# A hybrid decoder block in f32: a new order for the opening, for the weights at two stage borders, and for the gates

## The chip, the cores and the metric

The kernel runs on one core of one Trainium2 chip. The metric is the time of one execution on the device in microseconds (us), lower is better. Its engines are named as in the profile: PE (TensorE, with PEld for its weight loads), DVE (VectorE), ACT (ScalarE), POOL (GpSimd) and SP (SyncE, which here only issues loads and stores).

## The reference

One layer on 512 tokens of width 1024, all in f32: a gated feed-forward block (inner width 2816), a mixer, and a second feed-forward block, each with a norm ahead of it and behind it.

```python
f = swiglu(rmsnorm(x, ffn1_pre_g[l]), ffn1_w_gate[l], ffn1_w_up[l], ffn1_w_down[l])
x = x + 0.5 * rmsnorm(f, ffn1_post_g[l])
y = hybrid_mixer(rmsnorm(x, mix_pre_g[l]), positions, w_in[l], conv_w[l], conv_b[l], ...)
x = x + rmsnorm(y, mix_post_g[l])
f = swiglu(rmsnorm(x, ffn2_pre_g[l]), ffn2_w_gate[l], ffn2_w_up[l], ffn2_w_down[l])
x = x + 0.5 * rmsnorm(f, ffn2_post_g[l])
```

Here `rmsnorm(x, g) = x * rsqrt(mean(x*x) + 1e-6) * g` along the width, and `swiglu` is `(silu(h @ w_gate) * (h @ w_up)) @ w_down`. The mixer projects `h` once and feeds two branches: windowed attention with 3 groups of 4 heads (window and dilation 128/1, 512/4, 2048/16; q and k partly rotated), and a matrix memory (mLSTM) with 4 heads, whose input and forget gates are 8 more columns of the projection. Both are gated, added and projected by `w_out`.

## The kernel before

Tokens stand in 4 tiles `x0` to `x3` of 128 tokens. A normed tile `h` is transposed on PE and kept as features by tokens, split in two f32r parts: `hTh`, a rounded copy made by ACT, and `hTl`, the rest, made by DVE (`turn_norm`). Weights are split alike (`load_w`): SP loads a tile `wf` of 128x1024 (512 KB), ACT casts it to `wh`, DVE makes `wl = wf - wh`. A product in full precision is three: `wh` with `hTh`, `wh` with `hTl`, `wl` with `hTh`. `wf` has 3 buffers, `wh` and `wl` 5 each, so a load waits until DVE has made the `wl` of three tiles earlier, and a cast until PE has used the `wh` of five tiles earlier.

*Opening.* `x0`, the gain `f1pre` (spread over 128 partitions by its load), `x1`, the first block's gate and up weights (`agu00`, `agu01`), `x2`, `x3` and the next weights are loaded in this order by SP. `prenorm_first` squares and sums a tile on ACT, POOL takes the power -0.5, DVE scales by it and the gain. 28 products on zeros (`warm`) run on PE ahead. Then tiles 0 and 1 are transposed and split; the products of the first two of 22 inner blocks run over half the tokens at a time (`by_halves`): block 0 on tiles 0 and 1, then, at the places in `FLUSH`, the transposes of tile 2 and, within block 1, those of tile 3; then both blocks on tiles 2 and 3. Blocks 0 to 3 are plain products; the rest use a scheme with seven products for eight (`seven`), which needs sums of quarters of `h` (`token_parts`).

*Stage borders.* In `down`, the last products of a feed-forward block (and of `w_out`) are finished token tile by token tile: `PostNorm.bank` squares each half of a tile out of PSUM on ACT, and `prenorm` makes the next stage's `h`. The transposes of tiles 0 and 1 for the next stage are taken from `todo` between the products of the last two tiles. The next stage starts `by_halves` in the same way, with its first weights from `load_w`; all but the first are held by `tc.issue_after` until the transposes' copies are done.

*Gates.* The 8 gate columns come with group 0's values (`gts`). `gates()` transposes them on PE, then works on 4 rows of 512: two activations, an exponential and a logarithm on ACT (with a table load between them, and one back), and nine steps on DVE, two of them scans. It stands ahead of the loop over heads 1 to 3; in this loop each head projects q and k for its three groups (`qk_proj`, with the rotation in `qk_evac` on DVE), while the head before is finished (`exchange`, `turn`, `values`), and then computes its scores (`scores`). `gates_turn()`, eight narrow transposes, stands in head 1. `hg` and `selr` are two small tiles loaded by POOL that share buffers with the gates' temporaries.

The order on each engine is fixed when the program is built: a scheduler places the instructions by its own estimates, under the data's dependences and the `issue_after` pins; each engine then works strictly through its list.

Of the kernel before, what the change touches and what calls it, by code (L numbers as in the profile page):

```python
# [10 lines left out]
F32 = mybir.dt.float32  # L11
# [5 lines left out]
P = 128  # L17
# [17 lines left out]
WARM = 28  # L35
# [4 lines left out]
def tile_hybrid_block(ctx: ExitStack, tc: tile.TileContext, a: dict):  # L40
# [30 lines left out]
    for i in range(WARM):  # L71
        nc.tensor.matmul(wbank[:, 0:256], lhsT=warm[:, 0:P], rhs=warm, start=True, stop=True)
# [4 lines left out]
    nc.vector.memset(nhalf, -0.5)  # L77

    def load_w(src, name, n=1024, after=()):
        wf = act.tile([P, WMAX], F32, tag="wf", bufs=3, name=f"wf_{name}")[:, :n]  # L80
        nc.sync.dma_start(wf, src)
        with ExitStack() as st:
# [3 lines left out]
            nc.scalar.copy(wh, wf)  # L86
# [17 lines left out]

    def square(src, ss, b, name, half=False):
        junk = act.tile([P, 512], BF16, tag="junk", bufs=1, name=f"jk_{name}{b}")
        nc.scalar.activation(junk, src, AF.Square, scale=(2 if half else 1) * D ** -0.5, accum_out=ss[:, b:b + 1])
# [12 lines left out]
    def prenorm(t, g, where, name):  # L120
# [9 lines left out]
        return h  # L130

    def prenorm_first(t, g, where, after=None):
        h = scratch(f"h_f1{t}", *where)
        ss = small.tile([P, 2], F32, tag="ss", name=f"s1_{t}")[:, 0:1]
        with tc.issue_after(after) if after else nullcontext():
            nc.scalar.activation(h, xs[t], AF.Square, scale=D ** -0.5, accum_out=ss)
        nc.vector.tensor_scalar(ss, ss, EPS, None, op0=ALU.add)
        r = rsqrt(ss, 1, f"f1{t}")
        for c in BANKS:
            nc.vector.scalar_tensor_tensor(h[:, c], xs[t][:, c], r, g[:, c], op0=ALU.mult, op1=ALU.mult)  # L140
        return h
# [55 lines left out]
    def down(n, chunk_src, get_x, post, finish, todo, name, accs=None, first=0, late=lambda: None):  # L197
# [14 lines left out]
        for t in range(NT):  # L212
            pn = post(t)
            for b in range(2):
# [33 lines left out]

    def token_parts(low, tmp, hTh, hTl, name):
# [4 lines left out]
        for j in (1, 0):  # L254
            for i in (1, 0):
                nc.vector.tensor_tensor(quad(hf, i, j), quad(hTh, i, j).bitcast(F32), quad(hTl, i, j).bitcast(F32),
                                        op=ADD)
# [320 lines left out]
    def ffn(pool, todo, first_w, hT, wgu, wdq, wd, post, finish, name, begin=None, pins=()):  # L578
# [23 lines left out]
        for f in range(EARLY, PLAIN):  # L602
            w = load_plain(f)
# [668 lines left out]
```

## Time and profile before

| | |
|---|---|
| median of 3 runs | 1360.0 us (1359.94 to 1360.92) |
| the profiled execution | 1361.59 us, its span 1359.8 us |
| TensorE's granted clock, mean | 0.996 |
| ACT, POOL busy | 44%, 2% of the span |
| DMA | 145.91 MB, mean 107 GB/s |

Times in the profile count from the span's first instruction. A row of the timeline gives start, duration, engine, source line, operation and operands; a number in brackets is the time that the engine sat idle before it, and what ended it. Rows of PE's products overlap a little with their successors, since products are pipelined. In the list of waits, a row names the waiting engine and line, what was waited for, the sum, the number of times and the longest. A line of the stretches gives the stretch, the busy time of PE, PEld, DVE, ACT and POOL with counts of instructions, and then PE's clock, the share of busy DMA engines and GB/s.

### The profile page before, as it was taken

What the parts mean: (1) busy time and instruction counts of PE and PEld (TensorE: products, weight loads), DVE (VectorE), ACT (ScalarE), POOL (GpSimd) and SP (SyncE); (2) the same over time, 40 slices, a digit from 0 to 9 for tenths busy, and PEclk for the clock granted to TensorE, in tenths of its full rate; (3) what the DMA queues carried; (4) which work ended last, traced back from release to release, by engine and by line L of the source; (5) the groups of instructions that cost most, each with busy time, mean ns of one, the idle gap of its engine ahead of it and who ended that gap; (6) DMA issues with size and microseconds to landing.
All of it is one profiled execution on the core that took longest, in us unless ns stands there. A gap on an engine that the chain in (4) does not pass through costs nothing.

```text
span 1359.8 us, 19896 instructions
## 1 busy us (share of the span) xinstructions
PE 1344.6 (99%) x7976; PEld 1202.8 (88%) x7976; DVE 968.4 (71%) x1482; ACT 601.7 (44%) x969; POOL 30.1 (2%) x52
## 2 busy tenths in 40 slices
PE   8999999999999999999999999999999999999998
PEld 7899999878899889888888888888889999998786
DVE  7789898896772885675756754333378798997983
ACT  5444444555633532435545443222264444444552
POOL 1000000000200000000000000000010000000000
PEclk8999999999999999999999999999999999999999
DMA  5333333654233222222222232233213233335541
GB/s 201 94 109 95 109 109 109 232 171 150 69 93 123 78 78 91 81 78 78 78 78 78 78 108 79 95 107 100 95 47 116 94 94 108 109 104 194 174 150 62
DMA packets 40829, 145.91 MB, mean 107 GB/s; under 512 B 4652, under 2 KB 4652, under 8 KB 40736
## 3 DMA queue, kind: packets, MB, share of 16 engines
q1 hardware_dynamic: 39600, 141.08, 31.7%
q0 software_dynamic: 1136, 3.56, 0.8%
q8 instruction: 62, 1.02, 0.3%
q14 instruction: 31, 0.25, 0.1%
HBM read 142.53 MB, written 2.10 MB: 106 GB/s over the span
## 4 chain that ended last, share of the span: by engine, by line
PE 89%; DVE 6%; ACT 2%; issue 2%; DMA 1%; SPq 0%; DVEq 0%; POOLq 0%; ACTq 0%
PE p L176 11%; PE qb_b L319 9%; PE qb_a L319 9%; PE pq L176 8%; PE pm L176 6%; PE qa_b L319 4%; PE qa_a L319 4%; PE acc_o L227 3%; PE pvo L991 2%; PE pvo L993 2%; PE pvo L992 2%; PE pg_a L186 2%; PE pq L186 2%; PE pg_b L186 2%; PE pg_a L176 2%; PE pg_b L176 2%
## 5 line engine op out<-in xcount | busy, mean ns | idle before, releaser
L176 PE MATMUL pq<-hTh_mx,wh_qk 128*128 128x512 f32 x160 | 63.2, 395 | 0.0
L176 PE MATMUL pq<-hTl_mx,wh_qk 128*128 128x512 f32 x160 | 62.4, 390 | 0.0
L88 DVE TENSOR_TENSOR wl_qk<-wf_qk,wh_qk 128x1024 fp32r<-128x1024 f32 x24 | 29.3, 1221 | 41.6 <-ACT wh_qk L86 31.3
L176 PE MATMUL pm<-hTh_mx,wh_mqk 128*128 128x512 f32 x128 | 50.3, 393 | 0.0
L991 PE MATMUL pvo<-wh_vo,hTh_mx 128*128 128x512 f32 x128 | 50.2, 392 | 0.0
L176 PE MATMUL pm<-hTl_mx,wh_mqk 128*128 128x512 f32 x128 | 49.9, 390 | 0.0
L176 PE MATMUL p<-hTh_mx,wh_gm 128*128 128x512 f32 x128 | 49.9, 390 | 0.0
L993 PE MATMUL pvo<-wl_vo,hTh_mx 128*128 128x512 f32 x128 | 49.8, 389 | 0.0
L176 PE MATMUL p<-hTl_mx,wh_gm 128*128 128x512 f32 x128 | 49.8, 389 | 0.0
L992 PE MATMUL pvo<-wh_vo,hTl_mx 128*128 128x512 f32 x128 | 49.8, 389 | 0.0
L86 ACT CAST wh_qk<-wf_qk 128x1024 fp32r<-128x1024 f32 x24 | 25.0, 1045 | 56.1 <-PE pw L739 28.8
L1144 DVE SCALAR_TENSOR_TENSOR t<-t,p 128x512 f32<-128x512 f32 x16 | 11.0, 688 | 42.7 <-PE p L176 42.7
L88 DVE TENSOR_TENSOR wl_mqk<-wf_mqk,wh_mqk 128x1024 fp32r<-128x1024 f32 x16 | 19.6, 1223 | 29.7 <-ACT wh_mqk L86 25.3
L176 PE MATMUL pq<-hTh_mx,wl_qk 128*128 128x512 f32 x160 | 39.6, 389 | 0.0
L882 DVE SCALAR_TENSOR_TENSOR z<-pm,cw,z 128x511 f32<-128x511 f32 (+2 forms) x48 | 35.3, 743 | 1.4 <-ACT z L880 0.9
L319 PE MATMUL qa_a<-hTl_f,wh_a 128*128 128x256 f32 x144 | 36.1, 283 | 0.0
L319 PE MATMUL qa_b<-hTl_f,wh_b 128*128 128x256 f32 x144 | 36.1, 283 | 0.0
L319 PE MATMUL qa_a<-hTh_f,wh_a 128*128 128x256 f32 x144 | 36.1, 283 | 0.0
L319 PE MATMUL qa_b<-hTh_f,wh_b 128*128 128x256 f32 x144 | 36.1, 283 | 0.0
L247 ACT CAST wh_a<-cd_a 128x1024 fp32r<-128x1024 f32 x18 | 18.9, 1050 | 38.9 <-DVE cd_a L247 38.9
L247 ACT CAST wh_b<-cd_b 128x1024 fp32r<-128x1024 f32 x18 | 18.9, 1050 | 37.8 <-DVE cd_b L247 37.8
L176 PEld LDWEIGHTS pq<-hTh_mx,wl_qk 128*128 128x128 f32 x160 | 30.0, 188 | 6.2
(677 smaller groups left out, 4421.1 us busy)
## 6 DMA issues: line engine op xcount, KB each, us to landing
wf_qk<-in_wqk SPq DMA_DIRECT2D x24, 512.0 KB, 3.7
B_a<-in_wdq SPq DMA_DIRECT2D x21, 512.0 KB, 4.1
B_b<-in_wdq SPq DMA_DIRECT2D x21, 512.0 KB, 3.9
g_a<-in_wgu SPq DMA_DIRECT2D x18, 512.0 KB, 3.8
u_a<-in_wgu SPq DMA_DIRECT2D x18, 512.0 KB, 3.8
g_b<-in_wgu SPq DMA_DIRECT2D x18, 512.0 KB, 3.8
u_b<-in_wgu SPq DMA_DIRECT2D x18, 512.0 KB, 3.7
wf_mqk<-in_wmqk SPq DMA_DIRECT2D x16, 512.0 KB, 3.3
```

Of the source, the lines that this page charges most:

```text
L86: nc.scalar.copy(wh, wf)
L88: nc.vector.tensor_tensor(wl, wf, wh.bitcast(F32), op=ALU.subtract)
L176: nc.tensor.matmul(out, lhsT=wt[:, k * P:(k + 1) * P], rhs=x[:, k, tok], start=n == 0, stop=n == len(terms) - 1)
L186: nc.tensor.matmul(outs[b][:, tok], lhsT=ws_[b][w][:, k * P:(k + 1) * P], rhs=x[:, k, tok], start=i + k + hf == 0, stop=hf == 1 and i == 2 ...
L227: nc.tensor.matmul(out, lhsT=x[:, tk], rhs=w[:, cs], start=first and n == 0, stop=last and n == 2, skip_group_check=True)
L247: self.last[eng] = getattr(getattr(nc, eng), fn)(*args, **kw).ins
L319: nc.tensor.matmul(out, lhsT=wt[:, i * P:(i + 1) * P], rhs=y[:, i, :], start=first and n == 0, stop=last and n == len(terms) - 1, skip_gro ...
L882: nc.vector.scalar_tensor_tensor(z[:, s:], src[:, :T - s], cw[:, ct, 3 - s:4 - s], z[:, s:], op0=ALU.mult, op1=ALU.add)
L991: nc.tensor.matmul(out, lhsT=hTh[:, k, tk], rhs=wh[:, cs], start=k == 0, stop=False)
L992: nc.tensor.matmul(out, lhsT=hTl[:, k, tk], rhs=wh[:, cs], start=False, stop=False)
L993: nc.tensor.matmul(out, lhsT=hTh[:, k, tk], rhs=wl[:, cs], start=False, stop=k == KD - 1)
L1144: nc.vector.scalar_tensor_tensor(t1[:, b, :], t1[:, b, :], 1.0, p2[b], op0=ALU.add, op1=ALU.mult)
```

## The change

There are three parts.

*Opening.* The gain is loaded as one row of 4 KB by ACT's queue, and PE spreads it: two f32 products of a column of ones with the row put it in PSUM on all partitions, from where DVE reads it for tiles 0 and 1; ACT copies it to SBUF for tiles 2 and 3. The order of ACT and DVE is written out with `Order`. The 28 products on zeros become 34: `WARM` asks for 12 ahead of the row's products, 6 behind them, 10 behind tile 0's transposes and 6 behind tile 1's; in the built program two of the second group stand with the first, 14 and 4.

```diff
-WARM = 28
+WARM = (12, 6, 10, 6)
...
-        load_x(0)
-        g_pre = gain(a["ffn1_pre_g"], "f1pre", eng=nc.sync)
-        load_x(1)
+        row = work.tile([1, D], F32, name="f1pre_row")
+        ones = work.tile([1, P], F32, name="ones_row")
+        nc.vector.memset(ones, 1.0)
+        nc.scalar.dma_start(row, a["ffn1_pre_g"].rearrange("(o d) -> o d", o=1))
...
+        fill(WARM[0])
+        gp = pair("g_f1pre")
+        for b, c in enumerate(BANKS):
+            nc.tensor.matmul(gp[b], lhsT=ones, rhs=row[:, c], start=True, stop=True)
+        fill(WARM[1])
...
+        ss = [opening_square(t) for t in range(2)]
+        opening_power(0, ss[0])
+        opening_scale(0, 0, gp[0])
+        opening_power(1, ss[1])
+        for t, b in ((0, 1), (1, 0), (1, 1)):
+            opening_scale(t, b, gp[b])
+        whs = [opening_cast(0)]
+        turned = opening_turn(0)
+        for x in turned:
+            opening_high(*x)
+        whs.append(opening_cast(1))
+        turned += opening_turn(1)
...
```

ACT's list from the first square on, before (`h_f10` and `h_f11` are tiles 0 and 1, `wh_agu00` and `wh_agu01` the first two weights, `pt_f10_0` a bank of transposes):

```order
L136 ACTIVATE h_f10_130,s1_0_131<-x0_114 128x1024
L136 ACTIVATE h_f11_152,s1_1_153<-x1_115 128x1024
L86 CAST wh_agu00_176<-wf_agu00_174 128x1024
L151 CAST hTh_f1_128<-pt_f10_0_138 128x4x128
L151 CAST hTh_f1_128<-pt_f10_1_139 128x4x128
L151 CAST hTh_f1_128<-pt_f11_0_160 128x4x128
L151 CAST hTh_f1_128<-pt_f11_1_161 128x4x128
L86 CAST wh_agu01_182<-wf_agu01_180 128x1024
L136 ACTIVATE h_f12_188,s1_2_189<-x2_116 128x1024
L136 ACTIVATE h_f13_196,s1_3_197<-x3_117 128x1024
```

The same place after the change:

```order
L248 ACTIVATE h_f10_132,s1_0_136<-x0_86 128x1024
L248 ACTIVATE h_f11_133,s1_1_138<-x1_87 128x1024
L248 CAST wh_agu00_150<-wf_agu00_102 128x1024
L248 CAST hTh_f1_130<-pt_f10_0_152 128x4x128
L248 CAST hTh_f1_130<-pt_f10_1_153 128x4x128
L248 CAST wh_agu01_174<-wf_agu01_103 128x1024
L248 CAST hTh_f1_130<-pt_f11_0_176 128x4x128
L248 CAST hTh_f1_130<-pt_f11_1_177 128x4x128
L248 ACTIVATE h_f12_134,s1_2_198<-x2_88 128x1024
L248 COPY g_f1pre_200<-g_f1pre_0_120 128x512
L248 COPY g_f1pre_200<-g_f1pre_1_121 128x512
L248 ACTIVATE h_f13_135,s1_3_203<-x3_89 128x1024
```

The cast of the second weight moved ahead of tile 1's copies, and the gain's two copies stand between the squares of tiles 2 and 3. On DVE, the first sum of `token_parts` (`aT_a` from `hTh` and `hTl`) now stands ahead of the first two `wl`, with tile 2's small addition; before, both stood behind them.

*Stage borders.* `down` takes a function `ahead`, which calls `load_w` for the next stage's first two weights; the norm's first half of the last token tile is then pinned behind the second weight's cast. The other early weights are pinned behind a square of the last tile as well.

```diff
-                pn.bank(accs[t], b)
+                if (t, b) == (3, 0) and ahead:
+                    with tc.issue_after(ahead(pins[2:])):
+                        pn.bank(accs[t], b)
+                else:
+                    pn.bank(accs[t], b)
             finish(t)
-        return pins[2:]
+        return pins[2:] + squares[-3:-2]
...
+        def ahead1(pins):
+            wq0.extend(load_w(a["wqk"][0, 0, b], f"qk00{b}", after=pins if b else ()) for b in range(2))
+            return last_cast[0]
```

ACT's list at the first border, before (`wh_qk001` is the mixer's second weight, `jk_pf130` and `jk_pf131` the squares of the last token tile's halves, `h_mx2` the scaling of tile 2):

```order
L151 CAST hTh_mx_3743<-pt_mx1_0_3825 128x4x128
L107 ACTIVATE jk_mx21_3801,ss_mx2_3798<-x2_116 128x512
L151 CAST hTh_mx_3743<-pt_mx1_1_3826 128x4x128
L107 ACTIVATE jk_pf130_3839,sp_f13_3812<-accb_a3_2865 128x512
L129 ACTIVATE h_mx2_3797<-h_mx2_3797,r_mx2_3805 128x512
L86 CAST wh_qk001_3920<-wf_qk001_3918 128x1024
L107 ACTIVATE jk_pf131_3854,sp_f13_3812<-accd_a3_2861 128x512
L86 CAST wh_qk010_3926<-wf_qk010_3924 128x1024
L86 CAST wh_qk011_3932<-wf_qk011_3930 128x1024
```

The same place after the change:

```order
L148 CAST hTh_mx_3758<-pt_mx1_0_3840 128x4x128
L114 ACTIVATE jk_mx21_3816,ss_mx2_3813<-x2_88 128x512
L148 CAST hTh_mx_3758<-pt_mx1_1_3841 128x4x128
L91 CAST wh_qk001_3862<-wf_qk001_3860 128x1024
L137 ACTIVATE h_mx2_3812<-h_mx2_3812,r_mx2_3820 128x512
L114 ACTIVATE jk_pf130_3866,sp_f13_3827<-accb_a3_2880 128x512
L114 ACTIVATE jk_pf131_3881,sp_f13_3827<-accd_a3_2876 128x512
L91 CAST wh_qk010_3941<-wf_qk010_3939 128x1024
L91 CAST wh_qk011_3947<-wf_qk011_3945 128x1024
```

The cast changed places with the first square. At the second border (`ahead2`) the list changes in the same way, with `wh_bgu01` and `jk_pmx30`. SP's list of loads is the same as before but for the gain.

*Gates.* `gates()` and the load of `hg` move into head 1, behind its `turn`, and `gates_turn()` into head 2.

```diff
-    gates()
...
         pT = turn(h - 1, sm)
         if h == 1:
+            gates()
+            hg = work.tile([P, 1, D], F32, tag="gain", bufs=2, name="hg")
+            nc.gpsimd.dma_start(hg[:, 0, :], a["mlstm_head_g"].partition_broadcast(P))
+        elif h == 2:
             gates_turn()
```

DVE's list in head 1, before, around the rotation of its group 2 (`qk_12`; `sw_120` and `sw_121` are the swapped parts for q and k; `ga`, `gb4`, `gc4`, `selr` and `Gl` are the gates' rows):

```order
L724 TENSOR_TENSOR sw_111_4886<-sw_111_4886,ropeS_3897 32x512
L88 TENSOR_TENSOR wl_qk210_5167<-wf_qk210_5163,wh_qk210_5165 128x1024
L725 TENSOR_TENSOR qk_11_4879<-qk_11_4879,sw_111_4886 32x512
L88 TENSOR_TENSOR wl_qk211_5173<-wf_qk211_5169,wh_qk211_5171 128x1024
L722 STREAM_SHUFFLE sw_120_4989<-qk_12_4988 32x512
L723 TENSOR_TENSOR qk_12_4988<-qk_12_4988,ropeC_3896 32x512
L724 TENSOR_TENSOR sw_120_4989<-sw_120_4989,ropeS_3897 32x512
L725 TENSOR_TENSOR qk_12_4988<-qk_12_4988,sw_120_4989 32x512
L88 TENSOR_TENSOR wl_qk220_5266<-wf_qk220_5262,wh_qk220_5264 128x1024
```

The same place after the change:

```order
L811 TENSOR_TENSOR qk_11_4868<-qk_11_4868,sw_111_4875 32x512
L1007 SCALAR_TENSOR_TENSOR ga_4690<-gc4_4692 4x512
L1010 SCALAR_TENSOR_TENSOR ga_4690<-gc4_4692,ga_4690 4x512
L1012 SCALAR_TENSOR_TENSOR gb4_4691<-gc4_4692,ga_4690 4x512
L1013 TENSOR_TENSOR gb4_4691<-ga_4690,gb4_4691 4x512
L1014 SCALAR_TENSOR_TENSOR gc4_4692<-gb4_4691 4x512
L93 TENSOR_TENSOR wl_qk211_5178<-wf_qk211_5174,wh_qk211_5176 128x1024
L1015 CAST selr_4693<-gc4_4692 4x512
L1017 TENSOR_TENSOR gb4_4691<-gb4_4691,gc4_4692 4x512
L1016 TENSOR_TENSOR Gl_4694<-gc4_4692,selr_4693 4x512
L808 STREAM_SHUFFLE sw_120_4994<-qk_12_4993 32x512
L809 TENSOR_TENSOR qk_12_4993<-qk_12_4993,ropeC_3923 32x512
```

The gates' steps now stand between the rotations of groups 1 and 2 of head 1; before, they stood ahead of group 1's, between the steps of group 0 and of `exchange`. On POOL, the load of `selr` moved from behind the mixer's tables to ahead of the first power of the norm behind the feed-forward block.

More of the change, by code (lines that the diff above doesn't have):

```diff
@@ L70, in tile_hybrid_block, with fill @@
     wbank = bank("warm")
-    for i in range(WARM):
-        nc.tensor.matmul(wbank[:, 0:256], lhsT=warm[:, 0:P], rhs=warm, start=True, stop=True)
+    def fill(n):
+        for i in range(n):
+            nc.tensor.matmul(wbank[:, 0:256], lhsT=warm[:, 0:P], rhs=warm, start=True, stop=True)
     ident = ids.tile([P, P], F32, name="ident")
@@ L195, in new_hT, with down @@
         return hTh, hTl
-    def down(n, chunk_src, get_x, post, finish, todo, name, accs=None, first=0, late=lambda: None):
+    def down(n, chunk_src, get_x, post, finish, todo, name, accs=None, first=0, late=lambda: None, ahead=None):
         pins = []
@@ L588, in close, with load_plain @@
             nc.vector.tensor_tensor(aT[:, f, :], pg[1], s, op=MUL)
-        def load_plain(f):
+        def load_plain(f, after=()):
             return [load_w(wgu[f, :, b * 1024:(b + 1) * 1024], f"{name}gu{f}{b}",
-                           after=pins if f < EARLY and f + b else ()) for b in range(2)]
+                           after=pins if f < EARLY else after) for b in range(2)]
         early = []
@@ new lines, in tile_hybrid_block, with opening_square, opening_power @@
+        fill(WARM[1])
+        do = Order()
+        hT1 = new_hT("f1")
+        hs = [scratch(f"h_f1{t}", *(hbuf + tbuf)[t]) for t in range(NT)]
+        rs = {}
+        tt = lambda *args: do("vector", "tensor_tensor", *args[:3], op=args[3])
+        def opening_square(t):
+            ss = small.tile([P, 2], F32, tag="ss", name=f"s1_{t}")[:, 0:1]
+            do("scalar", "activation", hs[t], xs[t], AF.Square, scale=D ** -0.5, accum_out=ss)
+            return ss
+        def opening_power(t, ss):
+            do("vector", "tensor_scalar", ss, ss, EPS, None, op0=ALU.add)
+            rs[t] = rsqrt(ss, 1, f"f1{t}")
@@ new lines, in tile_hybrid_block @@
+        pins = (do.last["scalar"],)
+        ss += [opening_square(2)]
+        g_pre = work.tile([P, D], F32, tag="gain", bufs=2, name="g_f1pre")
+        for b, c in enumerate(BANKS):
+            do("scalar", "copy", g_pre[:, c], gp[b])
+        ss += [opening_square(3)]
+        opening_power(2, ss[2])
+        first_w = [opening_low(b, whs[b]) for b in range(2)]
+        opening_power(3, ss[3])
+        for t in range(2, NT):
+            for b, c in enumerate(BANKS):
+                opening_scale(t, b, g_pre[:, c])
@@ L728, in tile_hybrid_block, with qk_proj @@
     qk_of = {}
-    def qk_proj(h, g):
-        w = [load_w(a["wqk"][h, g, b], f"qk{h}{g}{b}") for b in range(2)]
+    def qk_proj(h, g, after=()):
+        w = [load_w(a["wqk"][h, g, b], f"qk{h}{g}{b}", after=after) for b in range(2)]
         pq = pair(f"pq{h}{g}")
@@ L945, in tile_hybrid_block @@
         nc.gpsimd.dma_start(caus[:, 0, :], a["caus"])
-    hg = work.tile([P, 1, D], F32, tag="gain", bufs=2, name="hg")
-    nc.gpsimd.dma_start(hg[:, 0, :], a["mlstm_head_g"].partition_broadcast(P))
     for h in range(1, HEADS):
```

87 lines of the change are left out of this document (56 added, 31 removed).

## Prediction

> **What bounds the kernel now.** I read the page's busy times first, then TensorE's waits over the whole span, then the busy times in stretches of 20 us.
>
> ```profile
> PE 1344.6 (99%) x7976; PEld 1202.8 (88%) x7976; DVE 968.4 (71%) x1482; ACT 601.7 (44%) x969; POOL 30.1 (2%) x52
> PE pt_f L148 <- DVE h_f L140: 2.7, 2, 1.6
> PE pt L844 <- DVE sm L835: 0.8, 1, 0.8
> PE pq L186 <- ACT wh_qk L86: 0.5, 1, 0.5
> PE pg_b L186 <- ACT wh_bgu L86: 0.5, 1, 0.5
> 0.00:20.00 20.00, 15.21 (x86) 13.00 (x87) 11.61 (x21) 11.59 (x17) 3.84 (x10) 0.83 0.74 259
> ```
>
> TensorE (PE) is busy for 1344.6 of 1359.8 us, so the products themselves set the end and an edit can only win back PE's waits (total us, times, longest) or a low clock. The waits that this change aims at are few: those of the opening, 0.8 us before the transposes of the softmax tile `sm`, and 0.5 us at each of two handovers. The first 20 us are also the only long stretch with a low granted clock (0.83, third from the right).
>
> **The opening.** First the rows of before (start, duration, engine, line; in brackets the idle time ahead and what ended it), then PE's clock in two stretches of one microsecond (third number from the right, after it the DMA share and GB/s).
>
> ```profile
> 1.06 5.02 PE L72 MATMUL warm<-warm 128*128 128x256 bf16 x28 [1.06 <-DVE nhalf L77]
> 4.30 1.06 ACT L136 ACTIVATE h_f<-x 128x1024 f32<-128x1024 f32 x1 [2.29 <-DMA x<-in_x]
> 7.10 1.06 ACT L136 ACTIVATE h_f<-x 128x1024 f32<-128x1024 f32 x1 [1.64 <-DMA x<-in_x]
> 9.70 1.05 ACT L86 CAST wh_agu<-wf_agu 128x1024 fp32r<-128x1024 f32 x1 [1.45 <-DMA wf_agu<-in_wgu]
> 10.65 2.04 ACT L151 CAST hTh_f<-pt_f 128x512 fp32r<-128x512 f32 x4
> 12.26 2.08 PE L186 MATMUL pg_a<-hTh_f,wh_agu 128*128 128x256 f32 x8 [1.04 <-ACT hTh_f L151]
> 13.67 2.35 DVE L88 TENSOR_TENSOR wl_agu<-wf_agu,wh_agu 128x1024 fp32r<-128x1024 f32 x2
> 16.06 1.22 DVE L256 TENSOR_TENSOR aT_a<-hTh_f,hTl_f 128x1024 f32<-128x1024 f32 x1
> 18.90 2.07 PE L186 MATMUL pg_a<-hTh_f,wl_agu 128*128 128x256 f32 x16
> 18.90 1.05 ACT L86 CAST wh_agu<-wf_agu 128x1024 fp32r<-128x1024 f32 x1 [2.25 <-DMA wf_agu<-in_wgu]
> 21.60 2.15 PE L186 MATMUL pg_a<-hTh_f,wh_agu 128*128 128x256 f32 x16
> 23.59 1.03 PE L148 MATMUL pt_f<-ident,h_f 128*128 128x128 f32 x8
> 66.18 0.69 DVE L247 TENSOR_TENSOR uv_a<-qb_a,q_a 128x512 f32<-128x512 f32 x1 [3.62 <-PE qb_a L319]
> 11.00:12.00 1.00, 0.22 (x3) 0.00 (x0) 0.73 (x2) 1.00 (x3) 0.00 (x0) 0.79 1.00 410
> 18.00:19.00 1.00, 1.00 (x8) 1.00 (x8) 1.00 (x2) 0.10 (x1) 0.20 (x1) 0.79 0.88 262
> ```
>
> *Loads.* The broadcast gain, 512 KB, leaves SP's queue. At 410 GB/s one such load takes 0.524 MB / 410 = 1.28 us, so every later load lands one slot earlier: the first weight, on which ScalarE (ACT) waited until 9.70, at 8.42.
>
> *First product.* ACT now runs cast, two copies of `hTh`, the second weight's cast, two copies. With the distances of before (a cast then 0.95 until the next, a copy 0.48) they start at 8.42, 9.37, 9.85, 10.33, 11.28 and 11.76. Before, the first product began 0.08 us after the third copy's end (10.65 + 2 x 0.48 + 0.57 = 12.18, against 12.26); now that copy ends at 11.85, and the product can start at 11.9. The 16 fillers and 16 transposes ahead of it fit: `x` of tile 1 is there at 5.8 and not 7.1, its `h` by about 9.3, and 8 transposes take 1.03.
>
> *Clock.* From 12.26 to 18.90 PE did 32 products, 0.207 us each; at full clock 16 take 1.92 (18.90 to the transposes at about 20.8), 0.120 each. The clock fell at 11.6 and rose at 18.4 (0.79 in both mixed stretches: 0.58 of the one and 0.59 of the other at full clock). If the fillers between the transposes keep it up, these 32 products take 3.83 us instead of 6.64 and PE asks for the low halves of the first weights at 15.7 rather than 18.90.
>
> *What is late next.* That does not reach the end whole, since VectorE (DVE) is not earlier. Its last `hTl` waits for the last copy (12.33) and ends at 13.2; then the order has an addition (1.22) and a small one (0.15) ahead of `wl` 0 and 1, so these run from about 14.4 to 16.75 and not from 13.67 to 16.0. PE hardly waits for them. But the load buffer of `wl` 0 is what the second block's second weight needs: before, `wl` 0 ended at 14.87 and ACT got that weight at 18.90, 4.0 us later. Now 15.6 + 4.0 = 19.6, the cast of 1.05 ends at 20.65, and PE's 8 products on it start at 20.7. Before they started at 22.55 (the second 8 of the 16 at 21.60, which end as the transposes at 23.59 begin). That is 1.85, and two products stand ahead of it that came behind before, 0.24: **2.1 us** won. Further on DVE waited for PE (3.62 us at 66.18), so it can follow and I let this gain travel to the end.
>
> *Not in the trace.* Two f32 products on a row of one partition, 1024 columns: between 0.48 (four times the 0.120 of 256 columns above) and 1.78 us (the row of L785 below, 8 f32 products of 128 columns, shown as 16); I take 1.78, the same operand type, or up to 3.6 at half clock. They start after 14 fillers of 0.207 at 3.96 and must end by 7.2, when DVE wants the second half: at most 0.4 us are uncovered. The row's load of 4 KB on ACT's queue: no earlier than 0, and by 4.30, when `x`, 128 times larger, had landed from the head of SP's queue; I take a landing before 3.96 and so no wait, against 0.34 at most. The gain read out of PSUM by DVE, and its two copies on ACT (about 0.57 each, like the copies above): they delay the square of tile 3 by 1.1 us, and DVE has that much other work then.
>
> **The two handovers.** Rows of ACT and PE at the first:
>
> ```profile
> 358.03 0.60 ACT L107 ACTIVATE jk_pf<-accb_a 128x512 bf16<-128x512 f32 x1
> 358.95 0.72 ACT L129 ACTIVATE h_mx<-h_mx,r_mx 128x512 f32<-128x512 f32 x1 [0.22 <-POOL r_mx L100]
> 359.57 1.03 ACT L86 CAST wh_qk<-wf_qk 128x1024 fp32r<-128x1024 f32 x1
> 360.51 0.59 ACT L107 ACTIVATE jk_pf<-accd_a 128x512 bf16<-128x512 f32 x1
> 360.66 1.22 PE L186 MATMUL pq<-hTh_mx,wh_qk 128*128 128x256 f32 x8 [0.55 <-ACT wh_qk L86]
> ```
>
> The cast moves to the place of the square at 358.03 and ends at 359.1; PE wants it at 360.1. The wait of **0.55** goes, and likewise **0.5** at the second handover. The squares follow the scaling of `h_mx`: from about 359.7 and 360.2, so the second, which frees the last tile's norm, is 0.3 earlier than now. If that cover failed, the cast's 1.03 would stand on the norm. SP's list is the same at both places, so nothing lands earlier: the weights were there, only ACT's turn was late. On POOL's queue the load of `selr` moves ahead of the first power of the norm, which comes one issue later for it; the products of three more token tiles cover that.
>
> **The gates.** Rows of ACT, DVE and PE, the last from the chain of waits:
>
> ```profile
> 449.19 0.66 ACT L920 ACTIVATE gc<-pgate,gb 4x512 f32<-4x512 f32 x1
> 452.26 0.62 ACT L922 ACTIVATE ga<-ga 4x512 f32<-4x512 f32 x1
> 452.90 1.28 ACT L923 ACT_TABLE_LOAD   x1
> 454.20 0.63 ACT L923 ACTIVATE ga<-ga 4x512 f32<-4x512 f32 x1
> 454.86 0.68 DVE L924 SCALAR_TENSOR_TENSOR ga<-gc,ga 4x512 f32<-4x512 f32 x1 [0.22 <-ACT ga L923]
> 456.07 1.21 DVE L926 TENSOR_TENSOR_SCAN gb<-gc,ga 4x512 f32<-4x512 f32 x1
> 478.55 0.72 DVE L722 STREAM_SHUFFLE sw<-qk 32x512 f32<-32x512 f32 x1
> 481.38 0.68 DVE L725 TENSOR_TENSOR qk<-qk,sw 32x512 f32<-32x512 f32 x1
> 483.99 0.71 DVE L722 STREAM_SHUFFLE sw<-qk 32x512 f32<-32x512 f32 x1
> 486.88 0.68 DVE L725 TENSOR_TENSOR qk<-qk,sw 32x512 f32<-32x512 f32 x1
> 444.28 1.04 PE L918 MATMUL pgate<-ident,gts 128*4 128x128 f32 x8
> 468.81 2.20 PE L844 MATMUL pt<-ident,sm 128*128 128x128 f32 x15 [0.77 <-DVE sm L835]
> 471.59 11.15 PE pq L176 x48
> 487.62 1.78 PE ps L785 x16
> ```
>
> Taking about 6 us of gate work off DVE between 450 and 462 makes `sm` ready near 462, so the wait of **0.77** at 468 goes. PE's 8 gate transposes (0.88: the row's 1.04 less its overlap with the next product) move behind it, so PE reaches the transposes of `sm` at 468.04 - 0.88 = 467.2, leaves them 2.20 later, at 469.4, and the gates' at 470.2. The next projection starts there and not at 471.59: 1.35 ahead, of which 0.58 (471.59 - 468.81 - 2.20) are eight narrow transposes that follow one head later. Then ACT's two activations end at 471.5, DVE's first gate step at 472.2, and DVE **stands at the second**, which needs exponential, table load and logarithm of ACT (0.62 + 1.28 + 0.63 and gaps, as from 452.26 to 454.83): until 474.8. Behind it in DVE's order stand the rest of the gates with one weight's low half: steps of 0.68, 1.21, 0.68, 1.21, 1.21, 0.41, 0.67 and 0.67 less overlaps of about 0.07, 6.2 us, to 481.1; then the rotation of q of head 1, group 2 (478.55 to 482.06 before: 3.5), a low half (1.21 less overlap), the rotation of k (483.99 to 487.56: 3.57). It ends at 489.2. PE, still 1.35 ahead, wants this k in the second half of L785: 487.62 + 0.89 - 1.35 = 487.16. So a new wait of **2.05 us** stands ahead of the last scores of head 1. Bounds: none, if DVE gets the 2 us back; 3.1, if its 15 steps behind ACT run without their overlaps of 0.07. I take the sum of rows. The waits at head 1's later steps start from the scores and have no row in before, so nothing more is added.
>
> The Trainium skill, "ScalarE: Activation LUTs", section "What ACT_TABLE_LOAD costs", puts a table switch at about 1.28 us plus a drain of 1.38. Here the logarithm starts at 454.20, 0.02 after the load of 1.28 ended, so the trace shows no drain; by the page's figure the wait would be 3.4 and the sum 1.4 us later.
>
> **The sum.** -2.1 (opening) - 1.05 (handovers) - 0.77 + 2.05 (gates) = -1.87 us. The profiled execution took 1361.59 us around its span of 1359.8; less 1.87 that is 1359.7 and 1357.9. The median of the runs shown is 1360.0, 1.6 below the profiled one; from it the forecast is **1358.2 us**.
>
> **Rivals.**
> - *No new wait at the scores.* For it: in before the k was done at 487.56 and wanted at 488.51, so 0.95 was free, and the wait is all made of DVE's 2.6 us behind ACT. Against: DVE's order is fixed, with the gates ahead of both rotations. Then -2.1 - 1.05 - 0.77 = -3.9: 1356.1.
> - *The opening wins more.* If the first weight also escapes the slow stretch ahead of it (its load took 2.6 us from 7.1 to 9.70, two slots), all steps up to the second weight move 1 us more: 1357.2. Against: a slow start shows at `x` too, 3.56 us for one load.
> - *The clock falls all the same.* Then PE starts at 11.9 at half rate until 18.4, 31 products, and is 0.26 ahead at the transposes of tile 2; in all -0.3 - 1.05 - 0.77 + 2.05 = 0: 1360.0. For it: in before it fell after some 5 us in which PE had only transposes. Against: from 8.6 to 11.6 there are now 16 fillers, 1.9 us at full clock, between them. The Trainium skill, "TensorE: Matmul & The Clock Gate", section "What's actually happening", says that the gate's window of about 3.4 us runs free of the kernel's start, so that the number of slow products varies from run to run. By that rule the fall would come in some runs of either kernel and the result would lie anywhere from 1358.2 to 1360.0; three runs of before within 0.98 us, with 2.8 us of slow products at stake, speak against a fall that comes and goes.
> - *The row lands late, and the kernel is slower.* PE stands in order behind the row's products from 3.96 on. Landing at 5.8, when `x` of tile 1 does, they run at half clock to 9.3; 4 fillers, 8 transposes and 10 fillers at half clock take 0.8, 2.1 and 2.1, to 14.3; with 8 transposes and a copy the first product comes at about 16.0 rather than 11.9; 48 products at 0.120 later PE is at 21.8 where before it was at 20.7. The opening then costs 1.1: 1.1 - 1.05 - 0.77 + 2.05 = +1.3: 1361.4. It decides from a landing at about 5.0 on.
>
> **How the numbers follow.** The forecast has 0.50; no new wait 0.20; the larger opening 0.12; the fallen clock 0.10; the late row 0.08. A measurement of this kernel tells 0.2%, 2.7 us, from no change, so 1357.3 and 1362.7 are the limits. Faster: the whole of the first rival, half of the second, and 0.06 of the forecast's own spread, 0.32. Slower: half of the late row and 0.02 for the handovers' cast on the norm, 0.06. The rest, 0.62, is no change. The range takes in the first rival with 0.4 to spare, the fallen clock and 0.4 above it: 1355.7 to 1360.4; the late row and the tail of a larger opening without a wait stay out.
>
> **What would show it.** In the changed kernel: clock 1.00 between 12 and 18 us; first product near 11.9; a wait of PE for ACT's cast of the second block's weight ending near 20.7; no wait at the handovers or at `sm`; and a wait of PE for DVE's `qk` of about 2 us at the line of the scores. No such wait refutes the gates' term; a clock of 0.50 refutes the opening's; a wait of the `g_f1pre` products for a DMA is the late row.

## The result, and the profile after

The changed kernel took **1363.74 us** (median of 7 runs, 1361.00 to 1365.52), the kernel before 1359.93 us on the same chip (7 runs, 1359.55 to 1360.92). The ratio is 1.0027, 95% interval 1.0018 to 1.0036: slower by 3.8 us. The forecast was 1358.2 with a range of 1355.7 to 1360.4, so the time lies outside it, on the other side. The profiled execution took 1365.52 us around a span of 1363.8, that is 4.0 more span than before (1359.8). It is the longest of the seven runs, 1.8 above their median, as the profiled execution of before stood 1.6 above its own; so the two profiles differ by as much as the medians, but neither is a typical run.

TensorE's waits over the span of the changed kernel (total us, times, longest):

```profile
PE ps L871 <- DVE qk L811: 3.6, 1, 3.6
PE warm L74 <- DVE warm L69: 1.1, 1, 1.1
PE accb_a L508 <- ACT xh_a L248: 0.6, 2, 0.4
PE accb_b L508 <- ACT xh_b L248: 0.6, 2, 0.4
PE pg_a L183 <- ACT wh_agu L91: 0.4, 1, 0.4
```

The waits at both handovers and ahead of `sm` are gone, as forecast. The new wait at the scores is there too, 3.6 and not 2.05. The row products of the gain do not wait for their load, so the rival of the late row does not apply. But the waits add up to less than before, and the kernel is slower, so time went into products that took longer. A ledger shows where: the start of the same piece of TensorE's work in the two profiled executions.

| work of TensorE | before | after | after − before |
|---|---|---|---|
| transposes of token tile 3, opening | 23.59 | 24.09 | +0.50 |
| first product for `qa_a` | 61.60 | 61.86 | +0.26 |
| last transposes behind the first handover | 365.56 | 365.09 | −0.47 |
| first projection of head 1 | 445.08 | 443.73 | −1.35 |
| transposes of `sm`, head 0 | 468.81 | 466.53 | −2.28 |
| projection behind them | 471.52 | 468.96 | −2.56 |
| first projection of head 2 | 489.16 | 491.15 | +1.99 |
| exchange of head 1 (`pe`) | 500.17 | 504.03 | +3.86 |
| projection behind the narrow transposes, now in head 2 | 513.52 | 518.14 | +4.62 |
| transposes behind the second handover | 1016.80 | 1020.71 | +3.91 |

Each handover won 0.7 (+0.26 to −0.47, +4.62 to +3.91). The gates first gain 2.1 by moving away (−0.47 to −2.56, of which 0.76 comes back later, +3.86 to +4.62), then cost 6.42 in head 1 (−2.56 to +3.86): 3.56 of waiting and 2.86 of something else. The opening won nothing.

**The 2.86.** The timeline of the changed kernel in head 1 (start, duration, engine, line), first the rows of ScalarE and VectorE, then those of TensorE:

```profile
469.72 0.66 ACT L1006 ACTIVATE gc<-pgate,gb 4x512 f32<-4x512 f32 x1
470.78 0.68 DVE L811 TENSOR_TENSOR qk<-qk,sw 32x512 f32<-32x512 f32 x1
471.39 0.67 DVE L1007 SCALAR_TENSOR_TENSOR ga<-gc 4x512 f32<-4x512 f32 x1
472.74 1.28 ACT L1009 ACT_TABLE_LOAD   x1
474.04 0.63 ACT L1009 ACTIVATE ga<-ga 4x512 f32<-4x512 f32 x1
474.70 0.68 DVE L1010 SCALAR_TENSOR_TENSOR ga<-gc,ga 4x512 f32<-4x512 f32 x1 [2.64 <-ACT ga L1009]
481.18 0.72 DVE L808 STREAM_SHUFFLE sw<-qk 32x512 f32<-32x512 f32 x1
488.62 0.68 DVE L811 TENSOR_TENSOR qk<-qk,sw 32x512 f32<-32x512 f32 x1
484.83 1.05 PE L871 MATMUL ps<-qk 128*128 128x128 f32 x8
489.45 2.04 PE L871 MATMUL ps<-qk 128*128 128x128 f32 x8 [3.56 <-DVE qk L811]
492.15 0.63 PE L173 MATMUL pq<-hTh_mx,wh_qk 128*128 128x512 f32 x1
495.37 0.39 PE L173 MATMUL pq<-hTh_mx,wh_qk 128*128 128x512 f32 x1
```

VectorE stands still for 2.64 until the logarithm is there, then does the gates, and its rotation of k ends at 489.30 while TensorE wants it at 485.89. After the wait the second half of the score products (four f32 products, shown as 8) takes 2.04 instead of 1.05, and a product of 512 columns shows 0.63 instead of 0.39. The busy times in stretches of 3.41 us say why (the second number is PE's busy time; the granted clock is the third from the right):

```profile
484.90:488.31 3.41, 0.99 (x9) 0.80 (x7) 3.38 (x5) 0.00 (x0) 0.00 (x0) 1.00 0.41 130
488.31:491.72 3.41, 2.27 (x10) 2.21 (x10) 3.34 (x14) 0.34 (x2) 0.00 (x0) 0.50 0.08 32
491.72:495.13 3.41, 3.41 (x9) 2.64 (x8) 1.84 (x11) 3.41 (x16) 0.00 (x0) 0.50 0.00 0
```

The idle stretch made the clock fall to half at 488.31, for 6.83 us, until 495.13. That cost is in no line of the waits. That it comes from the idle stretch, and not from something else at this place, is what experiment 4 tests.

**The opening.** The timeline of the changed kernel:

```profile
4.16 3.78 PE L664 MATMUL g_f1pre<-f1pre_row,ones_row 1*128 1x512 f32 x4
7.97 2.06 DVE L248 SCALAR_TENSOR_TENSOR h_f<-x,r_f,g_f1pre 128x512 f32<-128x512 f32 x3 [0.62 <-PE g_f1pre L664]
8.69 1.91 PE L689 MATMUL pt_f<-ident,h_f 128*128 128x128 f32 x8
10.40 2.34 PE L74 MATMUL warm<-warm 128*128 128x256 bf16 x10
12.53 1.69 PE L689 MATMUL pt_f<-ident,h_f 128*128 128x128 f32 x8
14.06 0.82 PE L74 MATMUL warm<-warm 128*128 128x256 bf16 x6
14.63 2.15 PE L183 MATMUL pg_a<-hTh_f,wh_agu 128*128 128x256 f32 x16
20.46 1.04 PE L145 MATMUL pt_f<-ident,h_f 128*128 128x128 f32 x8
23.04 1.22 PE L183 MATMUL pg_a<-hTh_f,wh_agu 128*128 128x256 f32 x8 [0.36 <-ACT wh_agu L91]
24.09 1.04 PE L145 MATMUL pt_f<-ident,h_f 128*128 128x128 f32 x8
```

The first product starts at 14.63, not 11.9, and the 8 products on the second block's second weight at 23.04, not 20.7 (before: 22.55). The row products take 3.78, eight transposes show 1.91 where the eight at 20.46 show 1.04, ten fillers take 2.13 (10.40 to 12.53, 0.21 each): everything ran at half clock up to 13.85, where the trace's record of the clock first rises. Stretches of the same kernel show a trap of the clock's column:

```profile
12.00:14.00 2.00, 2.00 (x12) 1.88 (x11) 0.00 (x0) 0.55 (x2) 0.00 (x0) 1.00 0.01 2
16.00:18.00 2.00, 2.00 (x19) 2.00 (x18) 2.00 (x4) 2.00 (x5) 1.15 (x1) 1.00 0.00 0
```

The clock column says 1.00 in both, but 12 instructions fit into the first stretch and 19 into the second. Before the first recorded change the column has nothing to show and prints full clock; the durations tell the truth.

### The profile page after: what moved, and what is told of

Read it like the earlier page. It is cut to its first block, busy times and chain, and to the rows that moved or that the text cites. A ratio compares the mean times of both kernels' runs of the same rounds, so it can differ in the third digit from the quotient of the medians.

```text
span 1363.8 us, 19918 instructions
## 1 busy us (share of the span) xinstructions
PE 1350.2 (99%) x7986; PEld 1206.1 (88%) x7986; DVE 969.0 (71%) x1483; ACT 602.9 (44%) x971; POOL 30.6 (2%) x52
## 3 DMA queue, kind: packets, MB, share of 16 engines
q0 software_dynamic: 1136, 3.56, 0.8%
## 4 chain that ended last, share of the span: by engine, by line
PE 89%; DVE 7%; issue 2%; ACT 1%; DMA 0%; DVEq 0%; POOLq 0%; ACTq 0%; SPq 0%
PE p L173 11%; PE qb_b L323 9%; PE qb_a L323 9%; PE pq L173 7%; PE pm L173 6%; PE qa_b L323 4%; PE qa_a L323 4%; PE acc_o L228 3%; PE pvo L1078 2%; PE pvo L1079 2%; PE pvo L1080 2%; PE pg_b L183 2%; PE pq L183 2%; PE pg_a L173 2%; PE pg_b L173 2%
## 5 line engine op out<-in xcount | busy, mean ns | idle before, releaser
L173 PEld LDWEIGHTS pq<-hTh_mx,wh_qk 128*128 128x128 f32 x160 | 30.8, 192 | 6.3
L173 PEld LDWEIGHTS pq<-hTl_mx,wh_qk 128*128 128x128 f32 x160 | 30.8, 192 | 6.2
```

The source lines that it names most:

```text
L173: nc.tensor.matmul(out, lhsT=wt[:, k * P:(k + 1) * P], rhs=x[:, k, tok], start=n == 0, stop=n == len(terms) - 1)
```

## The experiments

The experiments ran on four chips, on which the median of the kernel before lay between 1359.80 and 1360.24 us; so differences between experiments on different chips are good to a few tenths of a microsecond only. Two theories at the start. **G**: the gates' move makes the whole loss, by the late k and by the clock that falls over it. **O**: the opening's clock makes it.

**1. The gates back in head 0** (all else changed).

```diff
+    gates()
     nc.gpsimd.dma_start(selr[:, 0:512], a["sel"])
...
         if h == 1:
-            gates()
-            hg = ...
-        elif h == 2:
             gates_turn()
```

> The changed kernel with the gates back in head 0, so the new opening and the two handovers are all that is left of the change. Theory G (the gates make the whole loss: DVE is late with k of head 1 by 3.56 us, and the idle PE loses its clock for about 2.9 us more): from the two traces the opening stands 0.26 later and the handovers 0.73 and 0.71 earlier, so -1.18 us against the kernel before, about 1358.8 us; no wait of PE at the scores of head 1, clock 1.00 from 470 to 510, and runs that agree within about 1.5 us. Rival O (the loss and the spread of 4.5 us come from the opening's clock): the time stays at 1361 to 1365 and the spread stays.

Measured 1359.78 us (11 runs, 1358.45 to 1360.40) against 1360.24 (26 runs), ratio 0.9995 (0.9986 to 1.0004). Against the changed kernel that is −3.96: the wait of 3.6 is gone, 0.8 ahead of `sm` is back. So G holds for the larger part. (The change and this experiment, each taken against the kernel before beside it, are 4.3 apart.) But the runs fall into two groups, three at 1358.45 to 1358.84 and eight at 1359.50 to 1360.40, and the median is 1 us over the expectation: the opening seems to take one of two courses, by when its clock rises. The profiled execution was one of the three. Its clock rose at 4.30, fell at 7.72 and rose again at 11.13:

```profile
4.30:7.70 3.40, 2.72 (x11) 1.20 (x12) 1.33 (x4) 2.30 (x4) 0.84 (x2) 1.00 0.93 293
7.70:11.10 3.40, 3.40 (x19) 2.58 (x17) 2.98 (x5) 2.96 (x4) 0.27 (x1) 0.50 1.03 420
```

Its first product came at 12.56, and its first product for `qa_a` at 59.91, 1.95 ahead of the changed kernel's.

**2. The gates alone**, moved in the kernel before.

> The kernel before with nothing but the gates one head later. Theory G: the wait of PE for qk at the scores of head 1 is there, 2.5 to 3.6 us, and the 1.33 us of `sm` and the transposes are saved: +1.2 to +2.3 us in a run whose clock holds, 2.9 more where it falls: 1361.1 to 1365.0, with a spread of about 3 us between runs. Rival O: within 1 us of the kernel before, and as little spread as it has.

Measured 1363.72 us (7 runs, 1362.92 to 1366.62), ratio to before 1.0031 (1.0020 to 1.0041). One part of the change costs what the whole does. A line of its waits and one of its timeline:

```profile
PE ps L785 <- DVE qk L725: 3.6, 1, 3.6
59.54 0.28 PE L319 MATMUL qa_a<-hTh_f,wh_a 128*128 128x256 f32 x1
```

The clock fell here too, at 488.58, for one step of 3.41 and not two. This profile holds a second finding. Its opening is that of the kernel before, and in it the clock stayed full from 3.89 on: the first product for `qa_a` starts at 59.54, **2.06 ahead of the profile of before** with the same opening. The execution that I had predicted from was one with an unlucky clock.

**3. and 4. The wait filled with products** that nothing reads, between the halves of the second scores of head 1; 28 of them, then 14.

```diff
         for g in (1, 2):
+            for i in range(28 if (h, g) == (1, 2) else 0):
+                nc.tensor.matmul(ps1[0][:, P:2 * P], lhsT=q[1][:, 0, 0:P], rhs=q[1][:, 1, 0:P], start=True, stop=True)
             for j in range(NT):
```

> The changed kernel with 28 more f32 products of 128 columns (28 x 0.111 = 3.1 us at full clock) between the two halves of the second scores of head 1, in a part of the bank that the second half overwrites: PE's wait is filled with work that nothing reads. Theory G with the clock as a cost of its own: the k still comes at the same time, the wait shrinks to about 0.5 us, the clock stays 1.00 from 480 to 500, and about 2.9 us are won against the profiled run of the change: about 1361.0, spread 1.5 us. Rival (the wait alone costs it, or the clock falls for another reason): 1363.7 as the changed kernel, the clock at half after the scores.

Measured 1364.43 us (8 runs, 1363.44 to 1365.55). No verdict, since the filling was mis-sized: 56 instructions, 6.42 us, past the k (timeline of that kernel).

```profile
485.96 6.42 PE L870 MATMUL ps<-qk 128*128 128x128 f32 x56
```

> The run with filler products again, with half of them: a product with f32 operands shows as two instructions of 0.111 us, so 28 took 6.4 us and ran 2.6 us past the k. 14 of them take 3.1. Theory G with the clock as a cost of its own: PE waits at most 0.6 us after them, the clock stays 1.00 there, and 2.5 us less than with 28: about 1361.9 us, some 1.8 below the changed kernel though the k comes no earlier. Rival (the wait alone costs it): 1363.7 as the changed kernel.

Measured 1362.16 us (11 runs, 1360.79 to 1363.39), 1.6 below the changed kernel (1.8 if each is taken against the kernel before beside it, here 1360.16), 0.26 off the expectation. The timeline and one stretch of it:

```profile
484.94 3.29 PE L870 MATMUL ps<-qk 128*128 128x128 f32 x28
488.77 1.13 PE L873 MATMUL ps<-qk 128*128 128x128 f32 x8 [0.54 <-DVE qk L811]
```

```profile
488.30:491.70 3.40, 2.93 (x17) 2.64 (x18) 2.52 (x12) 1.00 (x5) 0.00 (x0) 1.00 0.00 0
```

The k comes no earlier by VectorE's order; TensorE still waits 0.54 for it. But the clock stays at 1.00, and from the projection ahead of the scores to the one behind them this kernel loses 3.83 on the kernel before (−3.34 to +0.49), where the changed one loses 6.42 up to the exchange. So the wait and the fall of the clock are two costs, and filling the idle time with useless products is worth 2.6 us in the profile.

**5. The gates late**, ahead of the second value projection, in the changed kernel.

```diff
-        if h == 1:
-            gates()
-            hg = ...
-        elif h == 2:
+        if h == 3:
             gates_turn()
         qk_proj(h, 2)
         values(h - 1, pT, v12)
         if h == 2:
+            gates()
+            hg = ...
             v12 = v12_proj(1)
```

> The changed kernel with the gates ahead of the second value projection (after head 2's turn, behind both rotations of its group 2; the narrow transposes in head 3), where PE has 96 products of 512 columns to do while DVE has little. Theory G: no wait at the scores of any head and none ahead of `sm` of head 0, so the opening's +0.26, the handovers' -1.44 and about -1.3 of the gates: -2.5 us, about 1357.4 us, faster than both kernels. Rival: the wait only moves, a wait of 1 to 3 us for DVE at the scores or at `sm` of head 2: 1358.4 to 1360.4.

Measured 1358.83 us (11 runs, 1356.76 to 1359.13), ratio 0.9986 (0.9977 to 0.9994): no wait at any scores, none ahead of `sm`. The place is good for the gates. The median is again over the expectation, and again three runs in eleven (1356.76 to 1357.21) stand 1.5 to 2 us ahead of the rest. The opening is left to explain.

**6. The old opening** with the handovers and the late gates.

> The kernel with the late gates and the two handovers, with the opening of the kernel before. Theory P (the new opening is no gain: in 3 of 4 runs its clock rises only near 13.6 us, 2.3 us of PE's time later than where the old opening has its clock from 3.4 to 4.8 us on and holds it): 1359.7 - 1.44 - 1.4 = 1356.8 us in most runs and up to 2 us more in a few; median about 2 us below the kernel with the new opening (1358.8). Rival (the new opening wins the forecast 2.1 us, and the loss lies elsewhere): 1360.9.

Measured 1357.35 us (11 runs, 1356.53 to 1358.02), ratio 0.9979 (0.9970 to 0.9988): 1.48 below experiment 5, which differs in the opening alone. The intervals of the two ratios overlap, but 8 of the 11 runs of experiment 5 lie above every run of this one. The new opening is a loss in the median, and the rival falls.

**7. Fillers of one row**, in the kernel before.

```diff
-        nc.tensor.matmul(wbank[:, 0:256], lhsT=warm[:, 0:P], rhs=warm, start=True, stop=True)
+        nc.tensor.matmul(wbank[:, 0:256], lhsT=warm[0:1, 0:P], rhs=warm[0:1, :], start=True, stop=True)
```

> The kernel before with its 28 filler products cut to one partition (1 row of weights and of data, the same 256 columns and the same time each). Theory K (a product on one row of the array does not count as work for the clock, and so the row products of 4.2 to 7.9 us did not raise it): no rise near 4.8, the clock at half until 15 to 19 us in every run, the fast course is gone: 1361 to 1362.5 us, none below 1360.5. Rival W (any product counts, and the change only had too short a run of fillers): the clock rises between 3.9 and 5.5 and the time is that of the kernel before, 1359.7 to 1360.3 in the median.

Measured 1359.73 us (11 runs, 1359.52 to 1360.77), ratio 0.9999 (0.9990 to 1.0008). The clock went nearly as theory K has it (no rise near 4.8, the first at 13.65), but the time is that of the rival. Timeline and stretches of that kernel:

```profile
1.06 6.15 PE L72 MATMUL warm<-warm 1*128 1x256 bf16 x28 [1.06 <-DVE nhalf L77]
12.28 1.82 PE L186 MATMUL pg_a<-hTh_f,wh_agu 128*128 128x256 f32 x8 [0.16 <-ACT hTh_f L151]
59.69 0.28 PE L319 MATMUL qa_a<-hTh_f,wh_a 128*128 128x256 f32 x1
```

```profile
3.41:6.83 3.42, 3.42 (x18) 2.25 (x16) 0.51 (x2) 1.15 (x2) 0.55 (x1) 1.00 1.03 367
10.24:13.65 3.41, 3.25 (x14) 2.85 (x15) 2.82 (x5) 3.41 (x7) 0.00 (x0) 1.00 0.93 382
```

A window filled to the brim with one-row products (18 in 3.42 us, so at half clock, though the column prints 1.00 there) did not raise the clock; the rise came behind a window of transposes and projections. And yet the first product starts at 12.28, as in before (12.26), where data and not the clock sets it. With the clock at half until 13.65 the first product for `qa_a` starts at 59.69, only 0.15 behind experiment 2 (clock full from 3.89 on) and 1.91 ahead of before (clock at half from 11.58 to 18.41). So fillers on all rows bought nothing over fillers on one row: what counts is the clock behind the first product, from some 13 us on.

**8. The row products on all 128 rows**, in the kernel of experiment 5: `ones` with zeros below row 0, and the gain's row in a tile of zeros.

> The kernel with the late gates, its row products made on all 128 rows: ones in row 0 of the weights, zeros below, and the row of the gain in a tile of zeros; the result is the same. Theory K: fillers and row products are now one stretch of work of 6 us, the clock rises by 7.4 us at the latest wherever the window lies, and all runs are on the fast course: about 1357.0 us, against 1358.8 with 3 fast runs in 11. Rival W: as before, median 1358.8 with one run in four near 1356.9.

Measured 1358.24 us (11 runs, 1356.80 to 1359.16), ratio 0.9985 (0.9976 to 0.9993). The median lies between the expectation and the rival, and the time decides nothing: clearing the tile held back the row's load, so that the products started at 6.68. But on the clock it completes experiment 7:

```profile
6.68 3.60 PE L665 MATMUL g_f1pre<-f1pre_row,ones_row 128*128 128x512 f32 x4 [1.60 <-DMA f1pre_row<-in_ffn_pre_g]
```

The window from 6.59 to 10.00 held these products alone (two in f32, shown as 4), and the clock rose at 10.00. The same two on one row raised nothing in the changed kernel.

**9. No fillers behind the row products** in the kernel of experiment 5: `WARM = (12, 0, 0, 0)`.

> The kernel with the late gates and the new opening, without the 22 fillers behind the row products and the transposes; the first 12 (14 as the trace counts) stay. Theory F (in the slow course the new opening is late because its row products and its 16 fillers between the transposes run at half clock, 0.207 us each, ahead of the first product): the first product comes at 12.3 to 12.9 us instead of 14.4, the stage at 60 us 1 to 2 us earlier, median about 1357.5 us against 1358.8. Rival H (the fillers hold the clock and pay for themselves): no gain, 1358.8 or later, with the clock at half until 15 us or more in every run.

Measured 1357.53 us (11 runs, 1355.71 to 1357.87), ratio 0.9980 (0.9971 to 0.9989): 1.3 below experiment 5, as expected (0.9 if each is taken against the kernel before beside it). The runs still form two groups, five at 1355.71 to 1356.45 and six at 1357.53 to 1357.87. The profiled execution is the fastest of the eleven, and its first product comes at 11.57, earlier than expected. Its timeline:

```profile
3.73 2.25 PE L664 MATMUL g_f1pre<-f1pre_row,ones_row 1*128 1x512 f32 x4
7.24 3.45 PE L689 MATMUL pt_f<-ident,h_f 128*128 128x128 f32 x16 [1.26 <-DVE s L248]
11.57 2.17 PE L183 MATMUL pg_a<-hTh_f,wh_agu 128*128 128x256 f32 x16 [0.89 <-ACT hTh_f L248]
20.20 1.22 PE L183 MATMUL pg_a<-hTh_f,wh_agu 128*128 128x256 f32 x8
```

**10. The old opening with 5 fillers** behind the transposes of tile 0, on the kernel of experiment 6.

> The kernel with the old opening, the two handovers and the late gates, and 5 more fillers behind the transposes of token tile 0, where PE stood idle for 1.45 us (8.67 to 10.12). Theory H (in the old opening a fall of the clock after the idle stretch from 7 to 12 us costs up to 1.5 us in some runs): the clock that rose by 7 us stays up in every run and all runs come at 1356.5 to 1356.9 us; median 0.6 below the 1357.35 of the kernel without them, spread under 1 us. Rival: the fillers run at half clock where the clock has not risen by then and PE reaches the second transposes 0.1 to 0.3 us later: 1357.4 as without.

Measured 1357.12 us (11 runs, 1356.68 to 1357.52), ratio 0.9978 (0.9969 to 0.9987). The median is 0.2 and not 0.6 below experiment 6, which is too little to tell; the spread is 0.84 instead of 1.49 us. The clock of its profile rose at 6.25 and did not fall. But its first product for `qa_a` starts at 60.20, 0.49 behind the profile of experiment 6 (59.71), whose clock stood at half from 10.34 to 13.75; it waits 0.5 for a weight's cast that did not hold up the other. So this pair does not show that the fall cost anything there. The two windows behind the rise:

```profile
6.25:9.66 3.41, 2.33 (x18) 1.54 (x16) 1.86 (x4) 1.36 (x3) 1.08 (x2) 1.00 0.96 324
9.66:13.07 3.41, 2.29 (x16) 1.90 (x17) 3.18 (x6) 3.41 (x6) 0.00 (x0) 1.00 1.01 414
```

**11. The new opening with no filler at all**: `WARM = (0, 0, 0, 0)`.

> The kernel with the late gates and the new opening, without any filler. Theory F (what counts in the opening is when the first product starts and the clock from there on; a clock that is up before 11 us is worth little): the row products run at half clock from the landing of the row, near 2 us, to about 5.8 us, DVE does not wait for them, the first product comes at 11.4 to 12.0 us, the clock rises one or two windows of 3.41 us after PE is busy without a break, between 12 and 16 us; all runs within 1.5 us, median 1356.6 to 1357.6, at or below the 1357.53 of the kernel with 12 fillers. Rival H (the fillers ahead are what brings the clock up in time): the clock stays at half until 16 us or later, no run below 1357.5, median 1358.5.

Measured 1357.25 us (10 runs, 1355.55 to 1358.33), ratio 0.9975 (0.9966 to 0.9985). The median is as theory F has it, with a spread of 2.8 instead of 1.5. The profiled execution was the slowest of the ten: its row landed at 2.85, its first product came at 12.57 behind ScalarE's copies and its clock rose at 16.58, both later than expected; the clock is the rival's, the median is not.

```profile
2.85 3.74 PE L664 MATMUL g_f1pre<-f1pre_row,ones_row 1*128 1x512 f32 x4 [2.85 <-DMA f1pre_row<-in_ffn_pre_g]
12.57 3.78 PE L183 MATMUL pg_a<-hTh_f,wh_agu 128*128 128x256 f32 x16 [1.64 <-ACT hTh_f L248]
```

Experiments 6, 9, 10 and 11 all beat both kernels, by 2.3 to 2.8 us against the kernel before; between them the intervals do not decide. Experiment 6 is among them, so no new opening is shown to beat the old one.

## Why the prediction was wrong, step by step

- **The baseline failed first.** The sum was made against a profiled execution of 1361.59 and then moved to the median of 1360.0. The opening's term consisted of winning back a clock that stood at half from 11.58 to 18.41. The median hardly has that loss: of the 26 runs of before beside experiments 1, 2, 3 and 5, six show a mean granted clock of 0.996, as the profiled one does, and take 1360.63 to 1361.68; the 17 at 0.998 and 0.999 take 1359.55 to 1360.59 (three at 0.997 lie between, 1360.32 to 1361.24). Experiment 2 puts the difference at 2.06 us in the profile. So most of the −2.1 had already been taken off with the 1.6 us between profile and median. (By its own numbers the forecast is 1360.0 − 1.87 = 1358.1, not 1358.2; nothing hangs on it.)
- **The opening, −2.1, was +1.48** (experiments 5 and 6). Its data path was worked out nearly rightly: in the fastest run without the later fillers (experiment 9) the first product comes at 11.57 and the second weight's products at 20.20 (forecast 11.9 and 20.7), and the first product for `qa_a` at 58.55. That is 3.05 ahead of the profile of before, but only 0.99 ahead of the old opening with a full clock (experiment 2). The step that failed is "If the fillers between the transposes keep it up": in the profile of the changed kernel the clock had not come up at all before 13.85. Fourteen fillers from 1.06 to 4.0 fill a window of 3.41 only where the window lies well, the row products behind them do not raise it, and ten of the later fillers then stand at 0.21 each on the path itself, with six more behind the rise. The uncovered time of the row products, "at most 0.4", was the 0.62 that VectorE waited.
- **The rival of the fallen clock** was dismissed by three runs of before within 0.98 us. That was too few: 26 runs show both courses. In the traces the clock changes in steps of 3.41 us, and kernels that begin alike differ in the first rise: 3.89 (experiment 2) and 4.76 us (before) with the old opening, and 4.14 (experiment 5), 4.30 (experiment 1), 12.08 (experiment 4), 13.43 (experiment 3) and 13.85 us (the changed kernel) with the new one. By the Trainium skill, "TensorE: Matmul & The Clock Gate", section "What's actually happening", the gate's window of about 3.4 us runs free of the kernel's start; the traces agree.
- **The handovers, −1.05, were −1.44** in the ledger (0.73 and 0.71): the mechanism was right, the size a little low.
- **The wait ahead of `sm`, −0.77, went** as forecast, and 0.56 more: the prediction took 2.20 from the start of the transposes of `sm` to the gates' transposes, from a row of before; in the changed kernel it is 1.64 (466.53 to 468.17).
- **The new wait, +2.05, was +3.56**: right in place and cause, mis-sized. I had VectorE's first gate step follow ScalarE's activations, 1.3 us after TensorE's next projection began. ScalarE was ready (470.38, projection from 468.96), but VectorE was still at the rotation of group 1 until 471.46, and began the gates 2.43 after the projection. That is 1.1 of the 1.5; the steps themselves came 0.2 longer, and k's end to the first product 0.15.
- **The clock's fall at the scores was missing**: 2.86 in the profile, 1.58 between the medians of the changed kernel and experiment 4, which still waits 0.54. The prediction watched the clock in the opening alone and priced a wait by its length.
- The table load that I weighed cost what its row said: the logarithm starts at 474.04, 0.02 after the load's end. The drain of 1.38 in the Trainium skill, "ScalarE: Activation LUTs", section "What ACT_TABLE_LOAD costs", is not in this trace, and a wait that came out longer than forecast is no support for it.

Together: 3.58 (opening) + 1.51 (wait) + 1.58 (clock) − 0.39 (handovers) − 0.56 (1.33 and not 0.77 won at `sm`) = 5.7, which takes the forecast −1.87 to the measured +3.8. That it closes to a tenth is partly luck: the opening and the clock are differences of medians, the clock's between two kernels that were not run side by side, and the other three come from one pair of profiles.

Open: why experiments 9 and 11 still have two groups of runs when their first product hardly depends on the clock, and how often each course comes. One profile of each kernel doesn't tell it. Of the kernel before, 16 of the 94 runs beside the experiments show the mean granted clock of 0.996, which is that of its profile; but the share varies by chip, from 1 of 21 to 7 of 33.

## What to carry to other kernels

Before you price a low clock or a stall that a profile shows, look whether the profiled execution is a usual one: a term that only an unlucky execution has is not to be won from the median. A wait of an engine whose clock follows its work costs its length and then the slow stretch behind it, which no list of waits shows; a handful of useless products, sized by the result that is waited for, can be worth more than they cost, as in experiment 4, and fillers ahead of work that waits for data anyway can be worth nothing, as in experiment 7. When a block of small steps moves, put it where the waiting engine has long work of its own, here ahead of 96 products, and behind everything that this engine will ask for next.

## What the hardware showed that I had not expected

- **One-row products did not raise the clock.** Windows of 3.41 us busy to the last with them left it at half (experiment 7, 3.41 to 6.83; experiment 11, 2.92 to 6.34; the changed kernel, 3.61 to 7.02, of which the first 0.55 are fillers); two f32 products on 128 rows raised it (experiment 8, 6.59 to 10.00). In experiment 1 the stretch from 4.30 to 7.70 was 80% busy, two thirds of it with row products, and the clock fell at 7.72.
- **The fall seems to go by the busy share of a window and not by the longest gap; the rise does so roughly.** The clock held through 1.93 us of idle time (experiment 2, ahead of 7.59; 1.65 of them in one window) and fell in experiment 6 after a window whose longest was 1.45. Leaving one-row products out, the clock rose after windows that were 83% (experiment 2, 0.48 to 3.89: 2.83 us), 90% (experiment 5, 0.72 to 4.14) and 95% busy (experiment 7, 10.24 to 13.65), and not after 67% (488.31 to 491.72 of the changed kernel) or 75% (0.20 to 3.61). At 80% it rose once (experiment 9, 0.90 to 4.32) and once did not (before, 11.58 to 15.00). It fell after 29% (484.90 to 488.31), 44% (8.17 to 11.58 of before) and 49% (6.92 to 10.34 of experiment 6), and held after 52 and 53% (experiment 2; the second, 7.30 to 10.72, had only transposes, so these count) and 67% (experiment 10). The limits in between are readings from single windows.
- A fall lasted whole windows: after the same wait of 3.6 us it was two windows in the changed kernel, where the wait reached into a second window and left it 67% busy, and one in experiment 2, where the next window was busy throughout (488.58 to 491.99).
